# Seven half-size block products in place of eight in the second feed-forward block of a streaming-encoder layer

## The chip, the cores and the metric

The kernel runs on one core of one Trainium2 chip. The metric is the time of one execution on the device in microseconds (us), given as the median of several runs. One profiled execution is shown beside it.

## The reference

One encoder layer on 512 tokens of width 1024 in float32: a gated feed-forward block (inner width 2816), a mixer (trailing means and a state-space scan), a second feed-forward block, each on a normed and modulated copy of the residual stream, and a last norm. The part that matters here is the second feed-forward block:

```python
def swiglu(h, w_in, w_out):
    a, b = jnp.split(h @ w_in, 2, axis=-1)
    return (jax.nn.silu(a) * b) @ w_out

h = modulate(rms_norm(x, g_ffn2[l]), mod[:, 2, 0], mod[:, 2, 1])
x = x + 0.5 * mod[:, 2, 2][:, None, :] * swiglu(h, w_ffn2_in[l], w_ffn2_out[l])
```

## The kernel before

Everything is held transposed: 128 features on the partitions, the 512 tokens along the free dimension. The width of 1024 is 8 contraction tiles, the inner width of 2816 is 22 inner tiles. Each matmul takes a 128x128 block of weights and 512 tokens.

A float32 product is made of three matmuls. Both operands are split into an upper part (rounded by a ScalarE cast to the type that TensorE reads) and a lower part (VectorE: the operand less its upper part); `mm3` (L225 to L228) adds upper x upper, upper x lower and lower x upper in PSUM. `put_split` (L230 to L232) is that split for activations. h stands in HH (upper) and HL (lower).

The program is a list of *units*. A unit names a piece of weights in memory (`src`, `cols`), the matmuls that use it (`mm`) and what follows (`post`). The loop at the end of the program goes through the list. At unit q it issues the load of unit q + 4 (`LA`) on SP's queue (L1025, into one of three `raw` buffers) and the split of unit q + 2 (`SA`: the ScalarE cast into `wh`, L1034, and the VectorE difference into `wl`, L1036, three buffers each), then the unit's matmuls, then its `post`. This order is each engine's program order; the engines run through their queues in order, and wait for each other by semaphores.

The second feed-forward block (`ffn`, stage number s = 2) is:

- `group6`: eight units, one for each contraction tile, which make the gate and value sides of inner tiles 0 to 2 in six PSUM banks at once. Between them stands the making of h, tile by tile (`make_h1`, `make_h2`: VectorE L210 scales and norms, ScalarE L214 makes HH, VectorE L219 makes HL). The first three units run by halves of the tokens, since the norm of the second half is late. The weight splits of the first three have their lower part on GpSimd.
- inner tiles 3 to 21, two units each (gate side, value side) of 8 x 3 matmuls. After the second, `gate_store` takes silu of the gate side (ScalarE L371), times the value side (VectorE L373), and splits the product into a slot of GHA, GLA or GC (ScalarE L231, VectorE L232).
- After each of four blocks of inner tiles (6, 6, 5 and 5) the eight *outward* units: each makes one tile of the output from the block's inner tiles, and `residual` (VectorE L417) adds it to the residual stream X. The last two of them are in `tail`, which works by halves of the tokens (256 columns) and interleaves the last norm.

The mixer's large tiles (PM, QM, TB, MM, MISC) and the buffers of the modulation weights (`ada`) are no longer used when this block starts; GpSimd has no work in it but the first two weight splits, a few sums of squares and a part of the last norm.

Of the kernel before, what the change touches and what calls it, by code (L numbers as in the profile page):

```python
# [10 lines left out]
F32 = mybir.dt.float32  # L11
F32R = mybir.dt.float32r
# [6 lines left out]
KT = 8  # L19
# [26 lines left out]
class Unit:  # L46
    def __init__(self, src, cols, mm, pre=None, post=None):
        self.src, self.cols, self.mm, self.pre, self.post = src, cols, mm, pre, post
        self.late = self.hold = self.pool_lo = False


@with_exitstack
def block_kernel(ctx, tc, a, out):
# [3 lines left out]
    adap = ctx.enter_context(tc.tile_pool(name="adap", bufs=2))  # L57
# [19 lines left out]
    def new_gslots():  # L77
        gc = big("GC", [P, 4, T], F32R, "GC")
        for f in range(6):
# [15 lines left out]
    ACC = big("ACC", [P, T])  # L95
    EPSC = big("EPSC", [P, 1])
# [21 lines left out]
    ada_tiles = {}  # L118

    def ada_load(n):  # L120
        t = adap.tile([P, 1024], F32, tag="ada", name="ada")
# [65 lines left out]
    def norm_sum(pc, cs=ALL):  # L187
        """1/rms of the tokens cs, a column per 128 tokens"""
# [9 lines left out]
    def norm_rows(pr, rc, cs=ALL):  # L198
        """the columns of rc as rows, on all partitions"""
# [7 lines left out]
    def make_h1(s, k, part):  # L207
# [6 lines left out]
        S.activation(out=HH[:, k, cs], in_=t[:, cs], func=AF.Identity, bias=shift_col(s, k))  # L214
        return t

    def make_h2(s, k, t, part):
# [4 lines left out]
        )  # L222

# [17 lines left out]
    def group6(s, src, post, pre0=None):  # L241
        """six output tiles at once, contraction tile by contraction tile"""
# [57 lines left out]
    def tail(s, src6, src7, nk, xs):  # L300
        """the last two tiles of a residual, by halves of the tokens, and the norm of the first half"""
# [113 lines left out]

    def residual(s, d, p, last, cs=ALL):
# [50 lines left out]
    class Later:  # L467
        """vector-engine calls, made at once or kept for later"""
# [49 lines left out]
    def v_reduce(x, n, wide):  # L518
        """x - k*pi/2 in [-pi/4, pi/4] and k"""
# [344 lines left out]
    def std_unit(src, xh, xl, nk, posts, nm=1, pre=None):  # L864
        """nm output tiles of nk contraction tiles each"""
# [149 lines left out]
    ffn(2, a["w_f2_6"], a["w_f2_in"], a["w_f2_out"])  # L1015
# [4 lines left out]

    def load(j):
        if j < len(wunits):
            u = units[wunits[j]]
            t = rawp.tile([P, 1024], F32, tag="raw", name="raw")
# [3 lines left out]
    def split(j):  # L1028
        if j < len(wunits):
            u = units[wunits[j]]  # L1030
            t = raws.pop(j)[:, 0:u.cols]
# [168 lines left out]
```

## Time and profile before

| | before |
|---|---|
| median of 3 runs | 1078.23 us (1076.22 to 1079.45) |
| profiled execution, span | 1076.3 us (its own run time is not listed apart from the span) |
| TensorE matmul busy | 1046.1 us, 97% of the span, 4832 matmuls |
| VectorE, ScalarE, GpSimd busy | 637.7, 346.2, 232.1 us |
| second feed-forward block | from about 688 us to the end |

How to read the profile: PE is TensorE's matmuls, PEld its weight loads, DVE VectorE, ACT ScalarE, POOL GpSimd, SP the engine that issues the loads. A row of a timeline has start, duration, engine, line, operation, output<-inputs, shape and count; in brackets stands the idle time of the engine ahead of it and what ended it. A row of groups has line, engine, operation, output<-inputs, shapes, count, then the busy time in us and the mean duration in ns, then the idle time ahead of them and what ended it. A row of a table by stage has the stage, its length, the busy time of PE, PEld, DVE, ACT and POOL with the number of instructions, the granted TensorE clock (1.00 is full), the DMA share and GB/s. The DMA part has the issue, its count, the size of one, and the median us from issue to landing.

### The profile page before, as it was taken

To read this page: it belongs to the slowest core of one execution; us is meant where nothing else is said; L and a number is where in the kernel's file an instruction comes from. 1 tells how busy PE (TensorE), PEld (TensorE's weight loads), DVE (VectorE), ACT (ScalarE), POOL (GpSimd) and SP (SyncE) were. 2 spreads that over 40 slices of the span, in tenths; PEclk is the share of its full clock that TensorE was granted. 3 is DMA by queue.
4 is the path that set the end of the run, shared out by engine and by line. 5 is a ranking of instruction groups with operands and counts; after the bars stand their busy time and mean duration, and the time that the engine had idled before them with its cause. 6 is when DMAs were issued, how large, how long until landed. Compare 5 with 4: busy or idle time off the path is not lost.

```text
span 1076.3 us, 12567 instructions
## 1 busy us (share of the span) xinstructions
PE 1046.1 (97%) x4832; PEld 854.3 (79%) x4832; DVE 637.7 (59%) x1007; ACT 346.2 (32%) x509; POOL 232.1 (22%) x199
## 2 busy tenths in 40 slices
PE   7899999999999999989999999999999999999995
PEld 6678888888888888877888888988888888888885
DVE  6965878999796456789713474464333343333334
ACT  5242222223223244633343333243222222222243
POOL 2400200399885322235500001300000000000002
PEclk8999999999999999999999999999999999999998
DMA  9565554564465222312233222232332233233222
GB/s 348 204 208 194 200 198 152 206 227 165 159 238 191 81 73 81 99 49 98 86 121 129 96 98 89 59 116 78 103 106 98 74 103 104 70 100 118 76 62 79
DMA packets 46318, 138.12 MB, mean 128 GB/s; under 512 B 5153, under 2 KB 9377, under 8 KB 46258
## 3 DMA queue, kind: packets, MB, share of 16 engines
q1 hardware_dynamic: 46082, 136.73, 37.9%
q8 instruction: 38, 0.62, 0.2%
q0 software_dynamic: 176, 0.59, 0.1%
q14 instruction: 22, 0.18, 0.1%
HBM read 134.15 MB, written 3.15 MB: 128 GB/s over the span
## 4 chain that ended last, share of the span: by engine, by line
PE 88%; DVE 9%; ACT 1%; issue 1%; DMA 1%; SPq 0%; DVEq 0%; ACTq 0%
PE ps L226 26%; PE ps L228 26%; PE ps L227 26%; PE ps L251 2%; PE ps L252 2%; PE ps L255 2%; DVE ev L476 1%; DVE ACC L319 1%; DVE U L768 1%; DVE TB L127 1%; DVE QM L127 1%; PE ps L713 1%; DVE ev L210 1%; PE ps L815 1%; DVE wl L1036 1%
## 5 line engine op out<-in xcount | busy, mean ns | idle before, releaser
L228 PE MATMUL ps<-HH,wl 128*128 128x512 f32 (+1 forms) x832 | 325.8, 392 | 4.5 <-DVE wl L1036 4.5
L226 PE MATMUL ps<-HH,wh 128*128 128x512 f32 (+1 forms) x832 | 326.5, 392 | 0.0
L227 PE MATMUL ps<-HL,wh 128*128 128x512 f32 (+1 forms) x832 | 325.6, 391 | 0.0
L1036 DVE TENSOR_TENSOR wl<-raw,wh 128x1024 fp32r<-128x1024 f32 (+3 forms) x189 | 224.6, 1191 | 144.0 <-ACT wh L1034 142.9
L1034 ACT CAST wh<-raw 128x1024 fp32r<-128x1024 f32 (+3 forms) x203 | 188.9, 934 | 261.4 <-PE ps L227 132.1
L228 PEld LDWEIGHTS ps<-HH,wl 128*128 128x128 f32 x832 | 156.4, 188 | 42.1 <-DVE wl L1036 5.4
L227 PEld LDWEIGHTS ps<-HL,wh 128*128 128x128 f32 x832 | 156.5, 188 | 36.5
L226 PEld LDWEIGHTS ps<-HH,wh 128*128 128x128 f32 x832 | 156.3, 188 | 36.7 <-ACT PM L709 0.2
L181 POOL TENSOR_TENSOR ACC<-ACC,ev 128x512 f32<-128x512 f32 x15 | 19.4, 1294 | 537.3 <-ACT ev L180 537.3
L226 PE MATMUL ps<-GHA,wh 128*128 128x512 f32 (+1 forms) x308 | 118.8, 386 | 0.0
L228 PE MATMUL ps<-GHA,wl 128*128 128x512 f32 (+1 forms) x308 | 118.0, 383 | 0.0
L227 PE MATMUL ps<-GLA,wh 128*128 128x512 f32 (+1 forms) x308 | 117.9, 383 | 0.0
L417 DVE SCALAR_TENSOR_TENSOR X<-ps,MOD,X 128x512 f32<-128x512 f32 (+1 forms) x78 | 55.0, 705 | 75.1 <-PE ps L228 75.1
L373 DVE TENSOR_TENSOR ev<-ev,ps 128x512 f32<-128x512 f32 x44 | 30.1, 685 | 105.7 <-PE ps L228 103.7
L127 DVE CUSTOM_DVE_ANT_0 ada<-ada,C,COL 128x1024 f32<-128x1024 f32 x50 | 74.8, 1496 | 0.0
L231 ACT CAST GHA<-ev 128x512 fp32r<-128x512 f32 x36 | 22.3, 621 | 157.7 <-DVE ev L373 140.2
L226 PEld LDWEIGHTS ps<-GHA,wh 128*128 128x128 f32 x308 | 57.8, 188 | 12.9 <-ACT PM L709 0.4
L251 PE MATMUL ps<-HH,wh 128*128 128x512 f32 (+1 forms) x180 | 62.2, 360 | 5.8 <-ACT HH L214 5.8
L228 PEld LDWEIGHTS ps<-GHA,wl 128*128 128x128 f32 x308 | 57.8, 188 | 12.6
L227 PEld LDWEIGHTS ps<-GLA,wh 128*128 128x128 f32 x308 | 57.8, 188 | 12.4
L252 PE MATMUL ps<-HH,wl 128*128 128x512 f32 (+1 forms) x180 | 60.9, 353 | 0.0
L251 PEld LDWEIGHTS ps<-HH,wh 128*128 128x128 f32 x180 | 34.6, 192 | 13.0 <-ACT HH L214 8.4
(172 smaller groups left out, 1148.4 us busy)
## 6 DMA issues: line engine op xcount, KB each, us to landing
raw<-w_f_in SPq DMA_DIRECT2D x76, 512.0 KB, 3.4
ada<-w_ada SPq DMA_DIRECT2D x50, 512.0 KB, 3.5
raw<-w_f_out SPq DMA_DIRECT2D x32, 384.0 KB, 3.2
raw<-w_f_out SPq DMA_DIRECT2D x32, 320.0 KB, 3.0
raw<-w_in SPq DMA_DIRECT2D x18, 512.0 KB, 3.6
raw<-w_f SPq DMA_DIRECT2D x16, 384.0 KB, 3.3
PM<-w_ada SPq DMA_DIRECT2D x8, 512.0 KB, 6.5
QM<-w_ada SPq DMA_DIRECT2D x8, 512.0 KB, 8.2
```

The source lines that it names most:

```text
L127: V.tensor_tensor_reduce(out=t, in0=t, in1=C, scale=1.0, scalar=bada[:, n:n + 1], op0=ALU.mult, op1=ALU.add, accum_out=MOD[:, n:n + 1],)
L226: E.matmul(pst, wh, xh, start=first, stop=False)
L227: E.matmul(pst, wh, xl, start=False, stop=False)
L228: E.matmul(pst, wl, xh, start=False, stop=last)
L231: S.copy(out=hi, in_=src)
L251: E.matmul(pst[m][:, cs], hi[:, w], xh, start=first, stop=False)
L252: E.matmul(pst[m][:, cs], lo[:, w], xh, start=False, stop=False)
L255: E.matmul(pst[m][:, cs], hi[:, w], xl, start=False, stop=k == KT - 1)
L373: V.tensor_tensor(out=g, in0=sl, in1=pb, op=ALU.mult)
L417: V.scalar_tensor_tensor(out=X[:, d, cs], in0=p[:, cs], scalar=MOD[:, s * 24 + 16 + d:s * 24 + 17 + d], in1=X[:, d, cs], op0=ALU.mult, op1 ...
L1034: S.copy(out=hi[:, 0:u.cols], in_=t)
L1036: eng.tensor_tensor(out=lo[:, 0:u.cols], in0=t, in1=hi[:, 0:u.cols].bitcast(F32), op=ALU.subtract)
```

## The change

Inner tiles 0 to 2 stay in `group6`, and tile 3 stays as it was. The 18 others go by pairs of inner tiles. For one side (gate or value) of one pair, and one pair of contraction tiles, the product is a 2x2 by 2x2 block product: two inner tiles, two contraction tiles, two halves of the tokens (256 columns). It takes eight half-size block products; here it is made of seven (the Strassen scheme in Winograd's form), each of them three matmuls of 256 columns.

For that, sums of blocks are needed on both sides:

- Of h, once: GpSimd also forms h in float32 (`HF`), and after every second contraction tile `h_sums` makes four sums of its 128x256 blocks on GpSimd and splits them (ScalarE, VectorE) into `sums`, held in the mixer's PM and QM.
- Of the weights, for each load: `half_units` loads 1024 columns (four blocks of two inner tiles by two contraction tiles, twice) into one of three job buffers `JR` (two halves of MISC, and ADA), and GpSimd makes four block sums in three instructions (512, 256 and 256 columns). `split1` splits the 1024 columns of four block operands into `wh`, `wl`; `split2` splits the 768 columns of the three others into one of three buffers in TB and MM.

A load gives two units: `mm1` (four block products, 24 matmuls) and `mm2` (three, 18 matmuls); the two loads of a side cover the eight contraction tiles. Between them `post1` combines the four sums in two PSUM banks (four VectorE operations, two ScalarE copies of 256 columns), and `mm2` adds its products on top of them. The list has the first two units of one side, then the last two of the side before. Outward units follow after sides 3, 9 and 15, for 6 inner tiles each; the last four inner tiles go in two pieces for four of the output tiles, around the last units. `split2` is issued 6 or 4 units ahead of its use (`lead`) in place of 2.

```diff
+        self.load = self.split = None
+        self.lead = SA
...
+        gslots["gc"] = gc
...
-    adap = ctx.enter_context(tc.tile_pool(name="adap", bufs=2))
+    ADA = big("ADA", [P, 2048])
...
+        if s == 2:
+            G.tensor_scalar(out=HF[k % 4][:, cs], in0=t[:, cs], scalar1=shift_col(s, k), scalar2=None, op0=ALU.add)
+            made[k] = made.get(k, 0) + cs.stop - cs.start
         return t
+
+
+    HF = [x[:, o:o + T] for x, o in ((C, 0), (C, T), (ADA, 1024), (ADA, 1024 + T))]
+    made = {}
+    sums = {}
+
+    def h_sums(kp):
+        if not sums:
+            sums["h"] = big("SH", [P, 4, 4, T // 2], F32R, "PM")
+            sums["l"] = big("SL", [P, 4, 4, T // 2], F32R, "QM")
+        t = ADA[:, 0:1024].rearrange("p (s t) -> p s t", s=4)
+        f0, f1 = HF[2 * kp % 4], HF[(2 * kp + 1) % 4]
+        a11, a12, a21, a22 = f0[:, HA], f1[:, HA], f0[:, HB], f1[:, HB]
+        G.tensor_tensor(out=t[:, 0], in0=a21, in1=a22, op=ALU.add)
+        G.tensor_tensor(out=t[:, 1], in0=t[:, 0], in1=a11, op=ALU.subtract)
+        G.tensor_tensor(out=t[:, 2], in0=a11, in1=a21, op=ALU.subtract)
+        G.tensor_tensor(out=t[:, 3], in0=a12, in1=t[:, 1], op=ALU.subtract)
+        put_split(sums["h"][:, kp], sums["l"][:, kp], t)
...
+        if s == 2 and k % 2 and made[k] == T and made[k - 1] == T and k // 2 not in made.setdefault("sums", []):
+            made["sums"].append(k // 2)
+            h_sums(k // 2)
...
+    def ffn_seven(s, w6, win, wout):
+        JR = [MISC[:, 0:2048], MISC[:, 2048:4096], ADA]
+        st8 = {}
+        njob = [0]
+        def post6(pst):
+            new_gslots()
+            t1 = big("J2A", [P, 4096], F32R, "TB")
+            t2 = big("J2B", [P, 2048], F32R, "MM")
+            st8["p2"] = [(t[:, o:o + 768], t[:, o + 768:o + 1536]) for t, o in ((t1, 0), (t1, 1536), (t2, 0))]
+            for f in range(3):
+                gate_store(f, pst[2 * f], pst[2 * f + 1])
+        group6(s, w6, post6)
+        def plain(f, ab, slot, hold):
+            def mm(hi, lo):
+                p = ps()
+                hold.append(p)
+                for k in range(KT):
+                    w = slice(k * P, (k + 1) * P)
+                    mm3(p, hi[:, w], lo[:, w], HH[:, k, :], HL[:, k, :], k == 0, k == KT - 1)
+            post = (lambda: gate_store(slot, hold[0], hold[1])) if ab else None
+            return Unit(win[ab], 1024, mm, None, post)
+        def operand(name, kp):
+            if name[0] == "S":
+                i = int(name[1]) - 1
+                return sums["h"][:, kp, i, :], sums["l"][:, kp, i, :]
+            k, cs = 2 * kp + int(name[2]) - 1, (HA, HB)[int(name[1]) - 1]
+            return HH[:, k, cs], HL[:, k, cs]
+        def product(out_, hi, lo, i, kl, kp, name, first, last):
+            w = slice(256 * i + P * kl, 256 * i + P * kl + P)
+            xh, xl = operand(name, kp)
+            for n, (w_, x_) in enumerate(((hi, xh), (hi, xl), (lo, xh))):
+                E.matmul(out_, w_[:, w], x_, start=first and n == 0, stop=last and n == 2, skip_group_check=True)
+        class Pair:
+            pass
+        def half_units(src, pr, kh):
+            job = {}
+            def load():
+                t = JR[njob[0] % 3]
+                job["n"], job["t"] = njob[0], t
+                njob[0] += 1
+                nc.sync.dma_start(out=t[:, 768:1792], in_=src)
+                c = t.rearrange("p (i w) -> p i w", w=256)
+                G.tensor_tensor(out=c[:, 1:3], in0=c[:, 4:7:2], in1=c[:, 3:5], op=ALU.subtract)
+                G.tensor_tensor(out=c[:, 0], in0=c[:, 6], in1=c[:, 1], op=ALU.subtract)
+                G.tensor_tensor(out=c[:, 7], in0=c[:, 5], in1=c[:, 0], op=ALU.subtract)
+            def split1():
+                hi = wp.tile([P, 1024], F32R, tag="wh", name="wh")
+                lo = wp.tile([P, 1024], F32R, tag="wl", name="wl")
+                put_split(hi, lo, job["t"][:, 0:1024])
+                return hi, lo
+            def split2():
+                hi, lo = st8["p2"][job["n"] % 3]
+                put_split(hi, lo, job["t"][:, 1280:2048])
+                return hi, lo
+            def mm1(hi, lo):
+                if kh == 0:
+                    pr.a, pr.b = ps(), ps()
+                h1, h2 = slice(0, 256), slice(256, 512)
+                for kl in range(2):
+                    kp = 2 * kh + kl
+                    one, end = kp == 0, kp == 3
+                    product(pr.a[:, h1], hi, lo, 3, kl, kp, "A11", one, end)
+                    product(pr.a[:, h2], hi, lo, 0, kl, kp, "S2", False, end)
+                    product(pr.b[:, h1], hi, lo, 2, kl, kp, "S3", one, end)
+                    product(pr.b[:, h2], hi, lo, 1, kl, kp, "S1", False, end)
+            def post1():
+                h1, h2 = slice(0, 256), slice(256, 512)
+                e = ev()
+                S.copy(out=e[:, h1], in_=pr.a[:, h1])
+                V.tensor_tensor(out=e[:, h2], in0=pr.a[:, h2], in1=e[:, h1], op=ALU.add)
+                V.tensor_tensor(out=e[:, h1], in0=pr.b[:, h1], in1=e[:, h2], op=ALU.add)
+                V.tensor_tensor(out=pr.a[:, h2], in0=pr.b[:, h2], in1=e[:, h2], op=ALU.add)
+                V.tensor_tensor(out=pr.b[:, h2], in0=pr.b[:, h2], in1=e[:, h1], op=ALU.add)
+                S.copy(out=pr.b[:, h1], in_=e[:, h1])
+            def mm2(hi, lo):
+                h1, h2 = slice(0, 256), slice(256, 512)
+                for kl in range(2):
+                    kp = 2 * kh + kl
+                    end = kp == 3
+                    product(pr.a[:, h1], hi, lo, 0, kl, kp, "A12", False, end)
+                    product(pr.a[:, h2], hi, lo, 1, kl, kp, "S4", False, end)
+                    product(pr.b[:, h1], hi, lo, 2, kl, kp, "A22", False, end)
+            u1 = Unit(src, 1024, mm1, None, post1 if kh else None)
+            u1.load, u1.split = load, split1
+            u2 = Unit(src, 768, mm2, None, pr.done if kh else None)
+            u2.load, u2.split, u2.lead = (lambda: None), split2, 4 if kh else 6
+            return u1, u2
+        def pair(n, slot):
+            pa, pb = Pair(), Pair()
+            def done_a():
+                pa.s = []
+                for p in (pa.a, pa.b):
+                    e = ev()
+                    S.activation(out=e, in_=p, func=AF.Silu)
+                    pa.s.append(e)
+            def done_b():
+                two = lambda x: x.rearrange("p (f t) -> p f t", f=2)
+                t, o, ol = (GHA, slot, GLA) if slot < 4 else (gslots["gc"], 0, None)
+                for e, p, cs in zip(pa.s, (pb.a, pb.b), (HA, HB)):
+                    g = ev()
+                    V.tensor_tensor(out=g, in0=e, in1=p, op=ALU.mult)
+                    if ol is not None:
+                        hi, lo = GHA[:, slot:slot + 2, cs], GLA[:, slot:slot + 2, cs]
+                    else:
+                        hi, lo = t[:, 0:2, cs], t[:, 2:4, cs]
+                    put_split(hi, lo, two(g))
+            pa.done, pb.done = done_a, done_b
+            r = []
+            for ab, pr in enumerate((pa, pb)):
+                us = [half_units(win[2 + 4 * n + 2 * ab + kh], pr, kh) for kh in range(2)]
+                r.append(([u[0] for u in us], [u[1] for u in us]))
+            return r
+        def out_unit(d, f0, f1, s0, hold, first=True, last=True, lastb=False):
+            def mm(hi, lo):
+                if first:
+                    hold.append(ps())
+                p = hold[0]
+                for i in range(f1 - f0):
+                    w = slice(i * P, (i + 1) * P)
+                    mm3(p, hi[:, w], lo[:, w], *gslots[s0 + i], first and i == 0, last and i == f1 - f0 - 1)
+            post = (lambda: residual(s, d, hold[0], lastb)) if last else None
+            return Unit(wout[d, :, f0 * P:f1 * P], (f1 - f0) * P, mm, None, post)
+        hold = []
+        units.extend([plain(3, ab, 3, hold) for ab in range(2)])
+        seq, n, slot = [], 0, 4
+        for n in range(9):
+            seq.extend(pair(n, slot))
+            slot = (slot + 2) % 6
+        outs = {3: (0, 6), 9: (6, 12), 15: (12, 18)}
+        hold = [[] for _ in range(4)]
+        for i in range(18):
+            units.extend(seq[i][0])
+            if i:
+                units.extend(seq[i - 1][1])
+            if i in outs:
+                f0, f1 = outs[i]
+                units.extend([out_unit(d, f0, f1, 0, []) for d in range(KT)])
+        units.extend([out_unit(d, 18, 20, 0, hold[d], True, False) for d in range(2)])
+        units.extend(seq[17][1])
+        units.extend([out_unit(d, 18, 20, 0, hold[d], True, False) for d in range(2, 4)])
+        units.extend([out_unit(d, 20, 22, 2, hold[d], False, True, True) for d in range(4)])
+        units.extend([out_unit(d, 18, 22, 0, [], lastb=True) for d in range(4, 6)])
+        tail(s, wout[6, :, 18 * P:], wout[7, :, 18 * P:], 4, lambda k: gslots[k])
...
-    ffn(2, a["w_f2_6"], a["w_f2_in"], a["w_f2_out"])
+    ffn_seven(2, a["w_f2_6"], a["w_f2_in"], a["w_f2_out"])
...
+    early = {}
+    for j, i in enumerate(wunits):
+        if units[i].lead != SA:
+            early.setdefault(j - units[i].lead, []).append(j)
...
     def load(j):
...
+            if u.load:
+                u.load()
+                return
...
     def split(j):
...
+            if j in ws:
+                return
+            if u.split:
+                ws[j] = u.split()
+                return
...
             load(q + LA)
             split(q + SA)
+            for j in early.get(q, ()):
+                split(j)
...
+            one = v[:, :, :, 3].transpose(2, 1, 0, 3).reshape(2, P, 1024)
+            two = v[:, :, :, 4:].reshape(2, 2, 2, P, 2, 9, 2, P).transpose(5, 4, 0, 3, 2, 6, 1, 7).reshape(36, P, 1024)
```

More of the change, by code (lines that the diff above doesn't have):

```diff
@@ L118, in block_kernel @@
     ada_tiles = {}
+    ada_slot = [0]
     def ada_load(n):
-        t = adap.tile([P, 1024], F32, tag="ada", name="ada")
+        t = ADA[:, 1024 * ada_slot[0]:1024 * ada_slot[0] + 1024]
+        ada_slot[0] ^= 1
         nc.sync.dma_start(out=t, in_=a["w_ada"][n])
@@ L1156, in pack @@
         d[n + "_6"] = ca(v[:, :, :, 0:3].transpose(0, 1, 3, 2, 4)).reshape(KT, P, 768)
-        d[n + "_in"] = ca(v[:, :, :, 3:].transpose(3, 2, 1, 0, 4)).reshape(2 * (NF - 3), P, 1024)
+        if n == "w_f1":
+            d[n + "_in"] = ca(v[:, :, :, 3:].transpose(3, 2, 1, 0, 4)).reshape(2 * (NF - 3), P, 1024)
+        else:
+            one = v[:, :, :, 3].transpose(2, 1, 0, 3).reshape(2, P, 1024)
+            two = v[:, :, :, 4:].reshape(2, 2, 2, P, 2, 9, 2, P).transpose(5, 4, 0, 3, 2, 6, 1, 7).reshape(36, P, 1024)
+            d[n + "_in"] = ca(np.concatenate([one, two], axis=0))
         d[n + "_out"] = ca(wo[0].reshape(NF, P, KT, P).transpose(2, 1, 0, 3)).reshape(KT, P, NF * P)
```

## The prediction

> **What bounds the kernel now.** I read the page's first and fourth parts, then the table by stage.
>
> ```profile
> span 1076.3 us, 12567 instructions
> PE 1046.1 (97%) x4832; PEld 854.3 (79%) x4832; DVE 637.7 (59%) x1007; ACT 346.2 (32%) x509; POOL 232.1 (22%) x199
> ...
> PE 88%; DVE 9%; ACT 1%; issue 1%; DMA 1%; SPq 0%; DVEq 0%; ACTq 0%
> ```
> ```profile
> 800.00:900.00 100.00, 100.00 (x431) 80.44 (x430) 35.99 (x40) 24.72 (x32) 0.00 (x0) 1.00 0.30 95
> ```
>
> TensorE holds 88% of the chain, and in the middle of the second feed-forward block (the stage row: PE, PEld, DVE, ACT, POOL, clock, DMA share, GB/s) it never pauses, VectorE is a third busy and GpSimd does nothing. Fewer TensorE cycles are worth their full time there, as long as the others stay hidden.
>
> **What the change takes away.** A matmul's listed duration holds its drain; its price is the distance between starts. From TensorE's timeline, thirty 512-column steps and then thirty 256-column steps, first and last row of each, every matmul with its own weight load:
>
> ```profile
> 1044.18 0.40 PE L226 MATMUL ps<-GHA,wh 128*128 128x512 f32 x1
> ...
> 1051.16 0.40 PE L226 MATMUL ps<-GHA,wh 128*128 128x512 f32 x1
> ...
> 1054.64 0.28 PE L226 MATMUL ps<-GHA,wh 128*128 128x256 f32 x1
> ...
> 1058.17 0.28 PE L226 MATMUL ps<-GHA,wh 128*128 128x256 f32 x1
> ```
>
> 6.98 / 30 = 0.2327 us and 3.53 / 30 = 0.1177 us: halves cost half. Before: 18 tiles x 2 x 8 x 3 = 864 matmuls x 0.2327 = 201.0 us. After: 9 pairs of tiles x 2 x 4 pairs of contraction tiles x 7 x 3 = 1512 x 0.1177 = 178.0 us. **Gain on TensorE: 23.0 us.** The outward products and residuals are the same in number; four more outward units split the same columns, and their loads are hidden: 0.
>
> **What it adds, per weight load.** The 36 loads stay 36. Each load (a "job") now gets three GpSimd sums (512, 256 and 256 columns), its 1024-column split, and a second split of 768 columns. Every two jobs (a "group": the gate or the value side of one pair of tiles) get post1, four VectorE adds and two ScalarE copies of 256 columns between the first units A, B (24 matmuls each) and the second ones C, D (18 each). On TensorE's queue stand A, B of a group, then C, D of the group before. Prices (groups by shape for the second feed-forward block; then GpSimd's for the whole run, one 256-column row of its timeline, the DMA part):
>
> ```profile
> L1036 DVE TENSOR_TENSOR wl<-raw,wh 128x1024 fp32r<-128x1024 f32 x38 | 46.5, 1226 | 49.7 <-ACT wh L1034 48.8
> ...
> L1036 DVE TENSOR_TENSOR wl<-raw,wh 128x768 fp32r<-128x768 f32 x21 | 20.0, 955 | 7.4 <-ACT wh L1034 7.3
> L373 DVE TENSOR_TENSOR ev<-ev,ps 128x512 f32<-128x512 f32 x22 | 15.1, 686 | 70.9 <-PE ps L228 69.6 <-ACT ev L371 1.3
> ...
> L232 DVE TENSOR_TENSOR GLA<-ev,GHA 128x512 fp32r<-128x512 f32 x16 | 11.1, 693 | 11.0 <-ACT GHA L231 11.0
> ...
> L417 DVE SCALAR_TENSOR_TENSOR X<-ps,MOD,X 128x256 f32<-128x256 f32 x6 | 2.9, 476 | 2.3 <-PE ps L228 2.3
> ```
> ```profile
> L1034 ACT CAST wh<-raw 128x1024 fp32r<-128x1024 f32 x38 | 39.8, 1049 | 74.7 <-PE ps L227 40.5 <-issue 33.5 <-ACT wh L1034 0.7
> L1034 ACT CAST wh<-raw 128x768 fp32r<-128x768 f32 x23 | 19.0, 832 | 37.0 <-PE ps L227 26.7 <-issue 10.2
> ...
> L231 ACT CAST GHA<-ev 128x512 fp32r<-128x512 f32 x16 | 9.9, 621 | 67.8 <-DVE ev L373 67.8
> ...
> L345 ACT COPY ev<-ps 128x256 f32<-128x256 f32 x1 | 0.4, 372 | 0.7 <-DVE MISC L434 0.7
> ```
> ```profile
> L786 POOL TENSOR_TENSOR PM<-ev 128x512 f32<-128x512 f32 x4 | 5.2, 1297 | 14.6 <-DVE ev L476 14.4
> ```
> ```profile
> 312.60 0.62 POOL L688 TENSOR_TENSOR MISC<-MISC 128x256 f32<-128x256 f32 x1
> ```
> ```profile
> raw<-w_f_in SPq DMA_DIRECT2D x76, 512.0 KB, 3.4
> ```
>
> A pair of tiles (two groups, 168 matmuls) is 19.8 us of TensorE. VectorE has for it 4 x (1.23 + 0.96) + 8 x 0.48 + the gate's 2 x (0.69 + 0.69) = 15.4 us, GpSimd 4 x (1.30 + 0.62 + 0.62) = 10.2. Each alone fits. But the two exclude each other, as the timeline of the first block shows:
>
> ```profile
> 225.02 2.08 POOL L669 TENSOR_TENSOR PM<-TB,MISC 128x512 f32<-128x512 f32 x1
> ...
> 226.13 2.06 DVE L1036 TENSOR_TENSOR wl<-raw,wh 128x1024 fp32r<-128x1024 f32 x1
> ...
> 227.07 2.03 POOL L670 TENSOR_TENSOR PM<-TB,MISC 128x512 f32<-128x512 f32 x1
> ...
> 228.11 0.74 DVE L417 SCALAR_TENSOR_TENSOR X<-ps,MOD,X 128x512 f32<-128x512 f32 x1
> ```
>
> A VectorE split that costs 1.23 alone takes 2.06 beside GpSimd, GpSimd's 1.30 becomes 2.03, while an op that reads PSUM (228.11) isn't held. Of the pair's work, splits and the gate's lower halves (10.1 us) and GpSimd's 10.2 must go in turn: 20.3 us, already past 19.8.
>
> **The ring of waits.** The job buffers are three. Job n+3 is loaded when job n's 768-split is done, and that split stands in VectorE's in-order queue behind others: in order come [A] split768, [B's end] post1, [C] split1024, [D] split1024, split768, [D's end, every second group] the gate. Followed round once, from a landed load to the same load of the next pair: two sums 2.0 (with a step between), cast 1.05, split1024 behind the next job's 1.30 sum 0.9 + 1.23, that job's second sum 0.62, cast 1.05, split1024 1.23, split768 0.96, gate 2 x (0.69 + 0.62 + 0.69) = 4.0, split768 behind a 1.30 sum 1.3 + 0.96, two dependent adds and the copy 0.96 + 0.37, cast 1.05 and split1024 1.23, the second job's two sums 2.0 (it could be loaded only after the last split768), cast 1.05, split1024 1.23, split768 0.96, transfer 3.4: **27.5 us a pair, 7.7 over TensorE's 19.8.** TensorE then waits at the third matmul of A (the first that reads the lower half), 2.6 us in one group, 3.5 in the next, and 1.5 in its B.
>
> Outward blocks stand after groups 3, 9 and 15. Eight units of 18 matmuls (33 us) let the buffers fill. Walked from full buffers, a stretch of six groups stalls 0, 0, 3.1, 2.7, 5.0, 2.7, and the outward unit behind it 3.0 (post1 is late): 16.5; twice that is 33. The first four groups and the last two lose about 1 each, and the last gate (4.0 us, covered by two outward units of 6 matmuls, 2.8 us) about 1. **Ring: +36 us.** Bounds: by the exclusion alone 9 x 0.5 = +5; all nine pairs at 7.7, +69. I take the walk, since each of its steps is a row.
>
> **The first eight units (group6).** After contraction tiles 1, 3, 5 and 7 the sums of h are formed: a GpSimd add of 0.62, four sums of 0.62 with 0.08 between, then ScalarE's cast 1.05 and VectorE's lower half 1.23, all in the middle of the in-order chain that makes h. That chain has no room. TensorE's and VectorE's timelines there:
>
> ```profile
> 705.01 0.39 PE L251 MATMUL ps<-HH,wh 128*128 128x512 f32 x1
> ...
> 709.20 0.40 PE L251 MATMUL ps<-HH,wh 128*128 128x512 f32 x1
> ```
> ```profile
> 705.62 0.47 DVE L210 SCALAR_TENSOR_TENSOR ev<-X,GS,ps 128x256 f32<-128x256 f32 x1
> ...
> 708.13 0.48 DVE L219 SCALAR_TENSOR_TENSOR HL<-ev,MOD,HH 128x256 fp32r<-128x256 f32 x1 [0.58 <-ACT HH L214]
> ...
> 709.73 0.47 DVE L210 SCALAR_TENSOR_TENSOR ev<-X,GS,ps 128x256 f32<-128x256 f32 x1
> ```
>
> A unit starts every 4.19 us, the chain makes a tile every 4.11, and the tile for 709.20 was ready at 708.61. An insertion delays the chain by 0.62 + 2.8 + 1.05 + 1.23 less some 0.5 that runs beside the last h pieces, 5.2 us. Walked through: 2.0 at unit 2's second half, 6.3 at unit 3 (its weight split waits behind the second sums), 3.7 at unit 6, 1.0 at the first plain unit. **+13 us**; bounds 0 (all covered) and 4 x 5.2 = 21.
>
> **Sum.** -23 + 36 + 13 = +26. The profiled execution shows a span of 1076.3 and no time of its own; its span is 1.9 under the median of the three timings, 1078.2. So 1102.3 by span, **1104 us** as a timing, slower by 2.4%.
>
> **The clock.** Pauses may cost more than their length. The stages of 1 us at the start of this block (same columns as above):
>
> ```profile
> 690.00:691.00 1.00, 0.64 (x6) 0.43 (x4) 1.00 (x1) 0.00 (x0) 1.00 (x1) 1.00 0.07 16
> 691.00:692.00 1.00, 0.57 (x4) 0.52 (x4) 0.77 (x2) 0.19 (x1) 0.10 (x1) 1.00 0.00 0
> 692.00:693.00 1.00, 0.67 (x6) 0.63 (x6) 0.48 (x1) 1.00 (x3) 0.00 (x0) 1.00 0.88 286
> ...
> 694.00:695.00 1.00, 1.00 (x7) 1.00 (x7) 0.65 (x1) 0.32 (x1) 0.96 (x1) 0.50 0.00 0
> ...
> 697.00:698.00 1.00, 1.00 (x9) 1.00 (x9) 0.67 (x2) 0.30 (x1) 0.00 (x0) 0.86 0.49 194
> ```
>
> Three microseconds with TensorE two thirds busy were followed by about 3.2 us at half clock, 1.6 us lost. The walk has 11 pauses of 2 us or more (four in each long stretch, three in the first units). In the ring the slowed matmuls mostly fall where VectorE is late anyway, so I count 0; if all counted it would be 11 x 1.6 = 18. The Trainium skill ("TensorE: Matmul & The Clock Gate", HAM oscillation) says that only idle gaps over some 3.4 us lower the clock; by that only the four pauses above 3.4 (3.5 twice, 3.7, 6.3) would, 4 x 1.6 = 6 us as an estimate, and the sum 1110. The rows above, with no gap so long, show the drop at less.
>
> **Rivals.** (1) *The ring is hidden*: the walk puts GpSimd and VectorE at their worst order; if they interleave better, pairs stay near the 20.3 of the exclusion. For it: VectorE's total is 15.4 of 19.8, ScalarE has room. Against: every wait is in-order. Then -23 + 5 + 13 = -5: 1073, faster. It decides at 22.3 us a pair or less (19.8 + 23 / 9), with the first units covered; with 13 lost there, at 20.9. (2) *All hidden*: -23 + 0 + 5 at most: 1055 to 1060; against it the 0.6 us of lead in the first units. (3) *The clock falls in each pause and it counts*: 1104 + 18 = 1122. (4) *Half-size matmuls don't cost half* when the weight loads (79% busy already) come twice as often: at 0.133 a matmul the gain is gone; against it the thirty rows at 0.1177, with a load each.
>
> **How the numbers follow.** Forecast 0.47, its own range 1088 to 1118; rival 3 0.17; rival 1 0.19, spread 1064 to 1080; rival 2 0.08; rival 4 0.02; mixtures that end between 1080 and 1088 0.07. Within 0.3% (3 us, about what a measurement of this kernel can tell from no change) falls 0.07, from rival 1 and the mixtures; faster 0.25; slower 0.68. The range 1068 to 1126 leaves out rival 2, a third of rival 1 and the top of rival 3.
>
> **What would show it.** Right: in the new profile TensorE idles before the first units' matmuls, released by VectorE's lower half; the first eight units grow from 21 us (705 to 726) by some 13; VectorE's splits average well over 1.23; a steady pair takes 25 to 29 us; SP's queue waits for VectorE's 768-split. Wrong: TensorE without pauses at 0.1177 a matmul (rivals 1, 2), or 256-column steps above 0.12 (rival 4). The weakest step is the order in which GpSimd and VectorE take turns.

## The result, and the profile after

The changed kernel takes 1118.14 us (median of 4, 1117.71 to 1119.91). The kernel before took 1077.39 beside it on the same chip (1076.22 to 1079.45). Ratio 1.0376, 95% interval 1.0360 to 1.0393: slower by 41 us where 26 were forecast. The profiled execution after ran 1119.91 us with a span of 1118.0, the same 1.9 us around the span that the forecast assumed. Spans grew by 41.7. Of the experiments below, one execution each of e_four and e_spread was slow throughout (3564 and 1569 us), and the ratios leave both out.

The page of the kernel after: span, busy time of the engines, shares of the chain.

```profile
span 1118.0 us, 14282 instructions
PE 1049.9 (94%) x5474; PEld 880.6 (79%) x5474; DVE 707.1 (63%) x1123; ACT 389.6 (35%) x589; POOL 371.2 (33%) x339
PE 66%; DVE 15%; ACT 5%; POOL 5%; DMA 5%; issue 4%; DVEq 0%; POOLq 0%; ACTq 0%; SPq 0%
```

TensorE held 88% of the chain and now holds 66%; the rest has gone to VectorE, ScalarE, GpSimd and transfers, in shares of 5 to 15%. TensorE is still listed as 94% busy, but where the time is lost no engine is full: in the first long stretch of the table below (75.7 us) TensorE's matmuls need 59.3 at full pace and VectorE is busy for 41.26. That is a bound by *waits that follow each other*, not by an engine.

The table by stage, first three stages of the kernel before (the first eight units, inner tile 3, and the end from the last half outward units on), then seven of the kernel after: the first eight units, tile 3, the first four groups, the two long stretches of six groups, the last two groups, the end.

```profile
688.40:726.00 37.60, 36.47 (x208) 32.07 (x207) 24.04 (x43) 16.95 (x28) 3.98 (x2) 0.95 0.32 101
726.00:737.20 11.20, 11.20 (x50) 9.00 (x48) 5.98 (x8) 5.25 (x8) 0.00 (x0) 1.00 0.34 114
1033.70:1076.30 42.60, 31.41 (x167) 26.72 (x165) 20.02 (x29) 18.01 (x32) 10.21 (x7) 0.88 0.23 73
```
```profile
687.50:741.00 53.50, 41.48 (x209) 34.92 (x207) 25.93 (x44) 18.48 (x30) 31.89 (x36) 0.84 0.21 69
741.00:755.30 14.30, 13.04 (x49) 10.09 (x50) 11.56 (x12) 8.66 (x12) 9.46 (x8) 0.88 0.15 41
755.30:796.80 41.50, 37.48 (x301) 35.86 (x299) 22.40 (x33) 16.23 (x26) 16.35 (x15) 1.00 0.28 92
831.00:906.70 75.70, 66.06 (x505) 63.01 (x503) 41.26 (x58) 27.49 (x43) 30.96 (x30) 0.95 0.26 86
940.90:1016.80 75.90, 64.65 (x506) 61.83 (x504) 41.28 (x58) 27.48 (x43) 31.20 (x30) 0.98 0.25 86
1051.00:1070.80 19.80, 19.80 (x169) 19.80 (x168) 12.10 (x20) 7.18 (x13) 5.51 (x6) 1.00 0.22 73
1077.90:1118.00 40.10, 25.80 (x126) 19.17 (x124) 18.94 (x33) 18.06 (x35) 10.33 (x7) 0.89 0.26 82
```

By the starts on TensorE's timeline (stages in the table are cut at round times, so lengths differ by some 0.1 us), with each matmul of the change at the forecast's 0.1177 us, the difference is accounted for like this:

| | forecast | measured |
|---|---|---|
| TensorE's cycles, 864 x 0.2327 to 1512 x 0.1177 | -23.0 | -23.0 (the unstalled last pair: 19.8 us for 168, 0.118 each) |
| first eight units (37.65 to 53.36) and tile 3 (11.2 to 14.37) | +13 | +15.7 + 3.2 |
| first four groups (300 matmuls, 35.3 at full pace) | about +1 to +2 | +6.2, and 0.7 in the outward block behind |
| two long stretches (504 matmuls, 59.3 at full pace) and the outward blocks behind them | +33 | +16.4 + 16.6, and 0.7 in each outward block |
| last groups and end | about +2 | +0.1, and +5.9 (20.5 over the matmuls' time; before 14.6) |
| start of the block | 0 | -0.8 |
| sum | +26 | +42.4 (spans: +41.7) |

Groups by shape, kernel after, the second feed-forward block:

```profile
L485 PE MATMUL ps<-HH,wl 128*128 128x256 f32 x72 | 22.9, 318 | 14.2 <-DVE wl L261 14.2
L485 PE MATMUL ps<-HH,wh 128*128 128x256 f32 x72 | 22.4, 311 | 9.7 <-ACT wh L260 9.6
L261 DVE TENSOR_TENSOR wl<-MISC,wh 128x1024 fp32r<-128x1024 f32 x24 | 29.4, 1225 | 42.9 <-ACT wh L260 42.5
L261 DVE TENSOR_TENSOR wl<-ADA,wh 128x1024 fp32r<-128x1024 f32 x12 | 17.0, 1416 | 18.6 <-ACT wh L260 18.2
L500 POOL TENSOR_TENSOR MISC<-MISC 128x512 f32<-128x512 f32 x24 | 35.3, 1470 | 109.6 <-DMA MISC<-w_f_in 109.6
```

TensorE waits for the lower half (VectorE) and, which the forecast did not list apart, for the upper half too (ScalarE's cast). GpSimd's sums wait 109.6 us for loads into MISC alone. The same block by waits: who waits for whom, total, times, longest; then SP's queue between the first four groups and the end of the second long stretch.

```profile
ACT ps L535 <- DVE ps L534: 39.9, 18, 3.3
ACT wh L260 <- POOL MISC L501: 33.3, 12, 3.4
```
```profile
SPq L498 <- DVE J2A L261: 136.8, 19, 12.7
SPq L498 <- DVE J2B L261: 36.7, 7, 8.9
```

A load waits for the 768-column split of the job three back, up to 12.7 us at a time. The chain of work in order of time, in the second pair of a long stretch (start, length, what; left out are the "issue" pieces, some of 0.03 us and less, and, between 871.5 and 875.5, the gate and a cast), shows the ring closed:

```profile
849.07 3.40 DMA MISC<-w_f_in
...
852.54 1.50 POOL MISC L500
...
854.11 0.75 POOL MISC L501
...
854.88 1.06 ACT wh L260
...
857.10 0.96 DVE J2B L261
...
858.13 4.32 DMA ADA<-w_f_in
...
862.52 1.30 POOL ADA L500
...
863.89 0.74 POOL ADA L501
...
864.70 0.73 POOL ADA L502
865.43 1.23 POOL MISC L500
...
866.73 1.59 POOL MISC L501
...
868.35 1.05 ACT wh L260
...
870.57 0.95 DVE J2A L261
...
875.53 1.93 DVE J2B L261
...
877.52 3.73 DMA ADA<-w_f_in
```

No TensorE row stands in it. From the load at 849.07 to the load at 877.52, four jobs later, is one turn, 28.45 us a pair, where 27.5 was forecast and 19.8 is TensorE's own. By the starts on TensorE the second and third pair of this stretch take 28.8 and 26.3, those of the other 28.9 and 27.0. Two transfers stand in a turn (3.40 + 4.32 = 7.7), where the forecast's ring had one, and seven GpSimd sums (1.50 + 0.75 + 1.30 + 0.74 + 0.73 + 1.23 + 1.59 = 7.8).

### The profile page after: what moved, and what is told of

Its sections match the earlier page's. It is cut to its first block, busy times and chain, and to the rows that moved or that the text cites. A ratio compares the mean times of both kernels' runs of the same rounds, so it can differ in the third digit from the quotient of the medians.

```text
span 1118.0 us, 14282 instructions
## 1 busy us (share of the span) xinstructions
PE 1049.9 (94%) x5474; PEld 880.6 (79%) x5474; DVE 707.1 (63%) x1123; ACT 389.6 (35%) x589; POOL 371.2 (33%) x339
## 4 chain that ended last, share of the span: by engine, by line
PE 66%; DVE 15%; ACT 5%; POOL 5%; DMA 5%; issue 4%; DVEq 0%; POOLq 0%; ACTq 0%; SPq 0%
PE ps L255 19%; PE ps L257 19%; PE ps L256 18%; PE ps L485 3%; DMA MISC<-w_f_in 3%; DMA ADA<-w_f_in 2%; DVE wl L1249 2%; POOL MISC L500 1%; PE ps L280 1%; PE ps L281 1%; PE ps L284 1%; ACT wh L260 1%; DVE ev L676 1%; DVE ev L215 1%; DVE J2A L261 1%
## 5 line engine op out<-in xcount | busy, mean ns | idle before, releaser
L1249 DVE TENSOR_TENSOR wl<-raw,wh 128x1024 fp32r<-128x1024 f32 (+4 forms) x157 | 181.9, 1165 | 86.7 <-ACT wh L1247 86.6
L257 PE MATMUL ps<-HH,wl 128*128 128x512 f32 (+1 forms) x544 | 212.8, 391 | 5.8 <-DVE wl L1249 5.8
L255 PE MATMUL ps<-HH,wh 128*128 128x512 f32 (+1 forms) x544 | 213.3, 392 | 1.0 <-ACT wh L1247 1.0
L1247 ACT CAST wh<-raw 128x1024 fp32r<-128x1024 f32 (+4 forms) x171 | 151.5, 893 | 175.6 <-PE ps L256 92.3
L256 PE MATMUL ps<-HL,wh 128*128 128x512 f32 (+1 forms) x544 | 212.4, 390 | 0.0
L257 PEld LDWEIGHTS ps<-HH,wl 128*128 128x128 f32 x544 | 102.8, 189 | 30.8 <-DVE wl L1249 7.2
L255 PEld LDWEIGHTS ps<-HH,wh 128*128 128x128 f32 x544 | 102.8, 189 | 24.8 <-ACT wh L1247 1.4
L256 PEld LDWEIGHTS ps<-HL,wh 128*128 128x128 f32 x544 | 102.8, 189 | 23.5
L280 PE MATMUL ps<-HH,wh 128*128 128x512 f32 (+1 forms) x180 | 64.0, 370 | 16.8 <-ACT HH L219 11.9
L132 DVE CUSTOM_DVE_ANT_0 ADA<-ADA,C,COL 128x1024 f32<-128x1024 f32 x50 | 74.8, 1496 | 0.0
L255 PEld LDWEIGHTS ps<-GHA,wh 128*128 128x128 f32 x308 | 57.8, 188 | 18.9 <-ACT wh L1247 7.0
L500 POOL TENSOR_TENSOR MISC<-MISC 128x512 f32<-128x512 f32 x24 | 35.3, 1470 | 109.6 <-DMA MISC<-w_f_in 109.6
L257 PEld LDWEIGHTS ps<-GHA,wl 128*128 128x128 f32 x308 | 57.8, 188 | 16.6 <-DVE wl L1249 4.1
L281 PE MATMUL ps<-HH,wl 128*128 128x512 f32 (+1 forms) x180 | 62.7, 362 | 0.6 <-DVE wl L1249 0.6
L485 PE MATMUL ps<-SH,wh 128*128 128x256 f32 x216 | 61.7, 286 | 0.0
```

The source lines that it names most:

```text
L132: V.tensor_tensor_reduce(out=t, in0=t, in1=C, scale=1.0, scalar=bada[:, n:n + 1], op0=ALU.mult, op1=ALU.add, accum_out=MOD[:, n:n + 1],)
L255: E.matmul(pst, wh, xh, start=first, stop=False)
L256: E.matmul(pst, wh, xl, start=False, stop=False)
L257: E.matmul(pst, wl, xh, start=False, stop=last)
L280: E.matmul(pst[m][:, cs], hi[:, w], xh, start=first, stop=False)
L281: E.matmul(pst[m][:, cs], lo[:, w], xh, start=False, stop=False)
```

## Experiments

All are edits of the changed kernel; each ratio is against the kernel before on the same chip, with its 95% interval. The theory is the ring (load, sums, splits, load again into one of three buffers). The rivals were TensorE itself at half size, the exclusion between GpSimd and VectorE alone, and the transfers alone.

**No loads and no sums after the first three jobs (e_stale).**

```diff
-                nc.sync.dma_start(out=t[:, 768:1792], in_=src)
+                if job["n"] < 3:
+                    nc.sync.dma_start(out=t[:, 768:1792], in_=src)
...
+                if job["n"] < 3:   # the three GpSimd sums likewise
```

> Left out: the loads and GpSimd sums of all jobs after the first three (the job buffers keep their contents); splits, matmuls and all else stay. Theory ring (the changed kernel's waits come from the cycle load, GpSimd sums, splits on VectorE, three job buffers): the 39 us of waits in the pair stages and the 2 us behind them go, the 18 us of the first units stay: 1075 to 1082. Rival TensorE (twice as many weight loads, or the lower clock, cost the time): no change, above 1110.

Measured 1082.18, ratio 1.0048 (1.0030 to 1.0066), at the upper end of the expected range. The loads and sums are worth 1118.14 - 1082.18 = 36.0 us. TensorE at half size isn't it. The pair stages and the outward blocks behind them, which lose 41 us in the table above, still lose 4.8 here.

**Only the sums left out (e_nosum)**, the loads stay:

> Left out: the GpSimd sums of the weights after the first three jobs; the loads stay. Theory ring: 2.0 + 0.9 + 0.62 + 1.3 + 2.0 = 6.8 us leave the cycle of 27.5, which comes to 20.7 a pair: 1080 to 1090. Rival exclusion alone (GpSimd and VectorE in turn are the bound, whatever the loads): all of it goes, 1075 to 1080. Rival transfer alone (a job buffer is loaded too late): little changes, above 1105.

Measured 1083.98, ratio 1.0047 (1.0031 to 1.0064).

**Only the loads left out (e_noload)**, the sums stay (they work on the weights of the first three jobs):

> Left out: the weight loads of all jobs after the first three; the GpSimd sums stay. Theory ring: the transfer of 3.4 us leaves the cycle, and a job's first sums no longer wait for the second split of the job three before: 1083 to 1100. Rival exclusion alone: sums and splits still take turns, 1112 to 1120. Rival transfer alone: 1075 to 1080.

Measured 1085.34, ratio 1.0073 (1.0053 to 1.0094). The first long stretch of the three kernels (stage table; e_stale, e_nosum, e_noload in this order):

```profile
823.00:884.60 61.60, 60.11 (x505) 59.67 (x504) 39.54 (x59) 27.83 (x44) 0.00 (x0) 1.00 0.00 1
```
```profile
824.80:886.40 61.60, 60.13 (x505) 59.63 (x503) 38.46 (x57) 27.30 (x43) 0.00 (x0) 1.00 0.33 105
```
```profile
823.80:886.80 63.00, 60.61 (x506) 59.79 (x505) 42.33 (x58) 27.58 (x44) 32.15 (x32) 1.00 0.00 1
```

75.7 us become 61.6 and 63.0: 20.5 and 21.0 a pair. The chain above would give much the same: a turn of 28.45 less its 7.8 of sums is 20.6, less its 7.7 of transfers 20.7. That agreement proves little, since e_stale, which loses both, takes the same 61.6 as e_nosum; what is left there is a pause of about 1 us, for the lower half of a split, in each of two groups. In e_noload GpSimd is as busy as before (32.15 us) beside the same splits, and the stretch is only 1.4 us longer than without the sums: the exclusion alone falls. In e_nosum the DMA moves all its bytes: transfers alone fall. Either cut opens the ring. (e_noload doesn't price the transfer by itself: without the load the first sums also need not wait for the split of the job three back.)

**The splits of the h sums after the first eight units, in buffers of their own (e_defer).**

```diff
-        put_split(sums["h"][:, kp], sums["l"][:, kp], t)
+    def h_split(kp):
+        put_split(sums["h"][:, kp], sums["l"][:, kp], sums["t"][kp])
...
+                if f < 2:          # after the gates of tiles 0 and 1
+                    h_split(f)
...
+        def post_plain():          # after tile 3's gate side
+            h_split(2)
+            h_split(3)
```

> The four sums of h keep their place on GpSimd but get a buffer each, and their splits (ScalarE cast, VectorE lower half) are issued after the first eight units, between the gates of the first inner tiles, in place of in the middle of the chain that makes h. Theory: the first units lost their 16 us because that chain waits in order for GpSimd and the cast; 1100 to 1106. Rival: GpSimd's h work shuts out VectorE there by the port alone; within 4 us of 1118.

Measured 1106.28, ratio 1.0264 (1.0245 to 1.0283), just above the expected range. The first eight units:

```profile
690.70:727.90 37.20, 35.57 (x208) 30.45 (x207) 26.33 (x42) 15.95 (x27) 33.04 (x33) 1.00 0.30 100
```

They take 37.2 in place of 53.4, with the same GpSimd work beside them (33.04 us against 31.89): it was the insertion of ScalarE and VectorE in the chain that makes h, not the shared ports. Of the 16.2 us and the 2.6 won in tile 3 only 12 reach the end. About 3 of them were a loss of the one profiled execution of the changed kernel: five others of these kernels have the same code up to there (e_stale, e_noload, e_four_look, e_post1, e_spread), and take 52.3 and 12.4 us for the two stages in place of 53.4 and 14.4. And the first four groups now take 46.2 us (41.5 after); the splits, moved to the front of the ring, probably delay its first jobs.

**A fourth job buffer (e_four, e_four_look).** MM takes a job buffer, and the third buffer of `split2` moves to the spare part of TB and to C.

```diff
-        JR = [MISC[:, 0:2048], MISC[:, 2048:4096], ADA]
+        JR = [MISC[:, 0:2048], MISC[:, 2048:4096], None, ADA]
...
-                t = JR[njob[0] % 3]
+                if njob[0] == 2:
+                    JR[2] = big("JRX", [P, 2048], F32, "MM")
+                t = JR[njob[0] % 4]
```

> A fourth job buffer (in the mixer's MM; the third buffer of the second split moves to spare space). Theory ring: a load no longer waits for the second split that stands behind the gate, so the transfer leaves the cycle in most turns; 15 to 30 us faster, 1088 to 1103. Rival exclusion alone: no change, 1114 to 1120.

Measured 1099.90, ratio 1.0199 (1.0182 to 1.0216). The stages are read from one more execution of the same kernel, e_four_look.

> The kernel with four job buffers once more, for its profile: 1099 to 1101, with waits of 1 us or less in the groups where the changed kernel has 1.5 to 4.

Measured 1099.72 (one execution). Its first long stretch:

```profile
825.50:894.90 69.40, 63.73 (x505) 62.41 (x505) 47.48 (x59) 27.91 (x44) 32.48 (x27) 0.95 0.26 86
```

GpSimd and VectorE do the same work, yet the stretch loses 10.1 in place of 16.4. A buffer more lets a load start a job earlier; this is the direct sign of a ring through the buffers. It does not open it whole, and the waits did not fall to 1 us or less as expected: two groups still lose 4.4 and 3.5, with one pause of 3.1. The order of VectorE's queue is the same, which may be why.

**The last copy of `post1` on VectorE (e_post1).** It needs only the second of the four adds, but stands on ScalarE behind a wait for the last (the 39.9 us of waits above), with the next casts behind it.

```diff
-                S.copy(out=pr.b[:, h1], in_=e[:, h1])
+                V.tensor_copy(out=pr.b[:, h1], in_=e[:, h1])
```

> The last copy of post1 goes from ScalarE to VectorE, so that ScalarE's cast for the next split doesn't stand behind VectorE's four adds. Theory ring: 0.4 us more on VectorE against some 1.2 us less ahead of a cast, once or twice a pair: 2 to 10 us faster, 1108 to 1116. Rival: VectorE's busy time is the bound; 18 x 0.4 = 7 us slower, 1125.

Measured 1111.70, ratio 1.0311 (1.0294 to 1.0328): 6.4 us for a change of engine. The long stretches go to 73.1 and 72.9.

**The outward units spread over two groups (e_spread)**, two ahead of the border, three at it, three a group later.

```diff
+            if i in outs:
+                f0, f1 = outs[i]
+                o = [out_unit(d, f0, f1, 0, []) for d in range(KT)]
+                units.extend(o[0:2])
+            if i - 1 in outs:
+                units.extend(o[5:8])
...
-                units.extend([out_unit(d, f0, f1, 0, []) for d in range(KT)])
+                units.extend(o[2:5])
```

> The eight outward units after groups 3, 9 and 15 are spread over two groups (2, 3 and 3 of them between the halves of the groups) and not put together. Theory ring: the buffers fill twice in a stretch, and each of the two long stretches loses 5 to 8 us in place of 16: 15 to 25 us faster, 1093 to 1103. Rival: the waits are a price of every pair whatever stands between them; within 4 us of 1118.

Measured 1120.20, ratio 1.0386 (1.0368 to 1.0403): a miss, 17 us and more above what I expected. One more group is free of waits and the later ones wait more: each long stretch still loses about 16. The run isn't a clean test of the spreading, though. At the stretches' borders (six places) a load here is issued ahead of the second split that reads the buffer before, which then takes the next load's weights: the amount of work is the same, but that split also has to wait for the later load. The clean pair is e_best_a and e_best_b below, with four buffers, where this doesn't happen: there the spread version is 2.5 us faster in the medians, with intervals that overlap.

**All four edits (e_all4).**

> All four together: splits of the h sums deferred, the copy of post1 on VectorE, outward units spread, four job buffers. Theory ring: 14 + 25 to 35 us of the 41 over the kernel before go, besides the 23 gained: 1062 to 1080, same as or faster than the kernel before. Rival exclusion: 1095 to 1105.

Measured 1081.71, ratio 1.0032 (1.0021 to 1.0043): 1.7 us above the expected range, and still a little slower than the kernel before. The four edits changed the time by -11.9 (defer), -18.2 (four), -6.4 (post1) and +2.1 (spread) alone, -34.4 in sum, and -36.4 together: they add up to within 2 us. None touches a matmul.

**Looking for a version that wins (e_best_a, e_best_b, e_best_c).** The first pair stage of e_all4 still lost 11.9 us, since the job buffer in MM isn't free until the last h sums are split (SP's queue waits 25.9 us there for VectorE's split). The best versions keep defer, post1 and four, and take that buffer for the fourth job in place of the third, issue the first h splits ahead of the gates, move the gate of tile 2 back (by one unit in a and b, two in c), and interleave the last outward units. e_best_a has the outward units as in the changed kernel, e_best_b and e_best_c spread them.

```diff
-        JR = [MISC[:, 0:2048], MISC[:, 2048:4096], ADA]
+        JR = [MISC[:, 0:2048], MISC[:, 2048:4096], ADA, None]
...
+            gate_store(2, *st8["pst"])   # in post_plain; e_best_c: one unit later
...
+        last = [out_unit(d, 20, 22, 2, hold[d], False, True, True) for d in range(4)]
+        whole = [out_unit(d, 18, 22, 0, [], lastb=True) for d in range(4, 6)]
+        units.extend([last[0], whole[0], last[1], whole[1], last[2], last[3]])
```

> Splits of the h sums deferred, the copy of post1 on VectorE and four job buffers, outward blocks as in the changed kernel. Besides, against the run with all four edits: the new buffer is used for every fourth job and not first for the third (it was not free at the start, and the first pair stages lost 12 us there), the sums of h are split ahead of the gates, and among the last outward units the short and the long ones alternate (4.7 us of waits for ScalarE there). Theory ring: the first stage loses 3 in place of 12, the last 2 in place of 5: 1068 to 1075, 3 to 10 us faster than the kernel before. Rival exclusion: what is left is GpSimd and VectorE in turn: 1078 to 1083.

> The same with the outward units spread over two groups. Theory ring, with four buffers: the walk leaves 3 to 5 us of waits in a long stretch, and spreading takes half of that: 1066 to 1074, up to 4 us below the unspread one. Rival: as with three buffers, spreading moves the waits and takes none away: within 2 us of the unspread one.

> As the spread version with four buffers, but the gate of inner tile 2 is issued one unit later, behind the split of the second pair load, so that ScalarE's cast for the second pair unit (which came 3.0 us late, behind a gate's cast that waited for VectorE) no longer waits: the first pair stage loses 1 in place of 4 us, 1072 to 1075, 0.3 to 0.6% faster than the kernel before. Rival: another split takes its place there, since VectorE's queue in that stage is full: no change, 1076 to 1078.

Measured 1078.79, 1076.29 and 1077.18; ratios 0.9999 (0.9989 to 1.0009), 0.9989 (0.9976 to 1.0003) and 0.9994 (0.9983 to 1.0005). None differs from the kernel before; all three expectations of a gain were missed, and the times of the rivals came for e_best_a and e_best_c. That of e_best_a (GpSimd and VectorE in turn are what is left) isn't shown by the time alone: the exclusion was worth 1.4 us a stretch in e_noload. In e_best_c the first pair stage loses 8.0 us where that of e_best_b loses 8.2; in place of a pause of 3.0 for a cast stands one of 2.2 for a lower half, as its rival said. The pair stages of e_best_b (the first; then the free run of five groups in each long stretch):

```profile
736.20:775.50 39.30, 33.88 (x265) 32.83 (x264) 31.19 (x36) 15.59 (x23) 24.23 (x18) 0.96 0.27 98
819.60:871.60 52.00, 50.03 (x421) 49.60 (x419) 42.34 (x51) 21.99 (x32) 28.18 (x22) 1.00 0.28 95
915.70:967.80 52.10, 50.08 (x421) 49.66 (x419) 42.39 (x51) 21.98 (x32) 28.48 (x23) 1.00 0.27 95
```

At 0.1177 a matmul they would take 31.1, 49.4 and 49.4. All pair stages together lose 13.7 us (8.2 of it the first), the end 5 against the kernel before, the outward units 1.9, and the first units give 0.4 back: -23 + 13.7 + 5 + 1.9 - 0.4 = -2.8, and its profiled span is 1072.8, 3.5 under before's (one of its faster executions: 1074.78, median 1076.29). In the medians of e_best_b and e_best_c 2.0 and 0.7 us are left, within the interval. With 81% of VectorE's time used in such a stage (42.34 of 52.00; before a third), the slack that TensorE's gain needs is small. What holds e_best_c is seen in its waits of TensorE in the whole block, the end included:

```profile
PE ps L494 <- DVE wl L265: 8.4, 6, 2.8
PE ps L259 <- ACT wh L1264: 5.4, 6, 1.4
```

Still the lower half of a split and, most of them at the end, the outward units' casts, at 12 places, none over 2.8 us.

## Why the prediction was right, and where its sizes were off

Sign and mechanism held. Against 1104 (own range 1088 to 1118, range 1068 to 1126) 1118 was measured: within the range, at the upper edge of the likeliest case. The missing time lies in the first units with tile 3, the first groups and the end.

- **Gain on TensorE, -23.0: held.** 19.8 us in the row 1051.00:1070.80 for 168 matmuls, loads included. Rival 4 falls.
- **Ring, +36: the mechanism held, the size was some 5 too small.** By the table the pair stages and the outward blocks lose 41 us, of which the loads and sums make 36.0 (e_stale); that this part alone equals the forecast's whole is luck. Mis-sized: "The first four groups and the last two lose about 1 each", by its sum two of the 36; the first four lost 6.9 with the outward block. The walk started from full buffers; the first groups start behind the first units, with splits queued, and the first two groups' A and B follow each other with no C and D between them, which is the likely reason. The walk of a long stretch came out in total (16.5; 16.4 and 16.6, with 0.7 behind), but not in its parts, so the closeness is partly luck too. By the starts the six groups of the first stretch lose 0.0, 0.9, 4.2, 4.8, 3.3 and 3.2, with pauses of 0.5 to 1.5 us, and the outward block 0.7; the walk had its first two free, 5.0 in the fifth, 3.0 in the outward unit, and pauses of 2 and more. e_nosum and e_noload show that the ring closes through sums and loads together, e_four that it goes through the buffers.
- **First eight units, +13: right place, too small.** 18.9 with tile 3 in the profiled execution, about 16 in the five others with the same code (52.3 and 12.4 against 37.65 and 11.2). (The sign "from 21 us (705 to 726)" counts only the last five of the eight units; all eight took 37.65.) An insertion is 4.1 + 1.2 = 5.3 us, as forecast (5.2); VectorE's timeline, the split of an h sum and its wait for the cast in brackets:

```profile
703.01 1.23 DVE L261 TENSOR_TENSOR SL<-ADA,SH 128x1024 fp32r<-128x1024 f32 x1 [4.09 <-ACT SH L260]
...
712.64 1.22 DVE L261 TENSOR_TENSOR SL<-ADA,SH 128x1024 fp32r<-128x1024 f32 x1 [4.05 <-ACT SH L260]
```

  The pauses of TensorE were 3.1 and 5.1, and then four of 1.1 to 1.7 up to the end of tile 3, against 2.0, 6.3, 3.7 and 1.0. What the walk left out is the slow clock (5.3 us of slowed matmuls in the first units and tile 3, 1.1 before; 2 us of it show in the length of tile 3) and tile 3 itself, whose weight splits stand behind the fourth insertion in ScalarE's and VectorE's queues.
- **The end, about 1: too small, 5.9.** The short outward units (6 matmuls, 1.4 us) don't cover the casts of their weights: 3.5 us of waits for casts and splits, against none before, and 1 us of slow clock. The forecast costed the gate there and counted these units' loads as hidden.
- **Clock, 0: right at the one place of the ring that can be compared, too small by 2 us in tile 3; not rival 3.** Below.
- **The exclusion was read right, its sign was not.** "VectorE's splits average well over 1.23" is wrong: 1225 ns in MISC, 1416 in ADA. GpSimd took most of the delay: its 512-column sum went from 1297 to 1470 ns. One place on VectorE's and GpSimd's timelines:

```profile
865.73 2.00 DVE L261 TENSOR_TENSOR wl<-ADA,wh 128x1024 fp32r<-128x1024 f32 x1 [4.29 <-ACT wh L260]
```
```profile
865.38 1.27 POOL L500 TENSOR_TENSOR MISC<-MISC 128x512 f32<-128x512 f32 x1
866.73 1.58 POOL L501 TENSOR_TENSOR MISC<-MISC 128x256 f32<-128x256 f32 x1
```

  The sum started first; the split, 1.23 alone, ends 1.08 us after it. The next sum, 0.74 alone, starts inside the split and ends 0.58 after it. Each finishes a little less than its own length behind the other. The Trainium skill ("SBUF — State Buffer", "Who interferes with whom") says that a VectorE instruction with two SBUF inputs contends with a GpSimd instruction that reads SBUF, and that the issue order decides who blocks. The trace agrees: at both places the one that came second was held. An average then tells only who usually comes second.
- **Signs that were named:** SP's waits for the 768-split (136.8 and 36.7 us), TensorE's for the lower half, a pair at 25 to 29 us (28.45): all there. Rivals 1 and 2 fall.

## What to carry to other kernels

When work that was TensorE's becomes preparation on other engines, busy shares don't price it (here 63%, 35% and 33%): follow one buffer round, from its load through every queue back to its next load, and compare that turn with the time that TensorE takes for the same work. A turn is opened where it is cheapest: another buffer (-18 us), one copy off a busy queue (-6), a preparation moved out of the chain that feeds TensorE (-12). If, with all of that, the saved cycles only come out even, the scheme isn't worth its memory and its extra operations.

## What the runs showed that I had not expected

**The clock falls after short pauses, but not every time, and in the ring a fall could cost nothing.** TensorE's timeline in the first long stretch (idle time ahead of a matmul in brackets), and a stage of 1 us there:

```profile
865.75 0.38 PE L485 MATMUL ps<-HH,wh 128*128 128x256 f32 x1 [1.36 <-ACT wh L260]
...
867.79 0.58 PE L485 MATMUL ps<-HH,wl 128*128 128x256 f32 x1 [1.54 <-DVE wl L261]
868.17 0.41 PE L485 MATMUL ps<-SH,wh 128*128 128x256 f32 x1
...
873.08 0.41 PE L485 MATMUL ps<-HH,wl 128*128 128x256 f32 x1
```
```profile
868.00:869.00 1.00, 1.00 (x5) 1.00 (x6) 0.00 (x0) 0.65 (x1) 0.92 (x2) 0.50 0.00 0
```

Two pauses of 1.36 and 1.54 us, two matmuls between them, and then 23 steps in 4.91 us, 0.213 each, at a granted clock of 0.50. The Trainium skill ("TensorE: Matmul & The Clock Gate", "HAM oscillation") ties the drop to idle gaps over some 3.4 us. Here none was that long. But the same place in the second long stretch has the same two pauses and no drop:

```profile
975.76 0.39 PE L485 MATMUL ps<-HH,wh 128*128 128x256 f32 x1 [1.49 <-ACT wh L260]
...
977.80 0.38 PE L485 MATMUL ps<-HH,wl 128*128 128x256 f32 x1 [1.54 <-DVE wl L261]
```
```profile
978.00:979.00 1.00, 1.00 (x10) 1.00 (x10) 0.00 (x0) 0.63 (x1) 0.92 (x2) 1.00 0.00 0
```

So the pauses alone don't decide; what does stays open. The two places also show what the slow clock costs. From their first pause on, the same 84 matmuls take 14.67 us with the clock down and 14.69 without: in the second TensorE then waits 2.57 us for the next weights, in the first the slowed matmuls fill that time. In the block the slowed steps (1.7 to 1.95 times the full pace) are 13.4 us longer than at full pace, against 1.1 before; 6.5 of it lies in the two long stretches (3.8 and 2.7), which lose nearly the same, 16.4 and 16.6. In tile 3 it counts: with slowed matmuls there the tile takes 14.4 us, in the five kernels with the same code and none 12.4.

**Leftovers are worth looking for.** The wait of a ScalarE copy for an add that it doesn't need (39.9 us in 18 waits, the next casts behind it) gave 6.4 us. The two write the two halves of one PSUM tile; whether the chip would need that wait was not tried, only the copy's place.
